# Two value passes in place of three, and the softmax's denominators on GpSimd, in a forgetting-attention stage

## The chip, the cores and the metric

The kernel runs on one core of a Trainium2 chip. The metric is the device time of one execution in microseconds, the median of several runs. TensorE (PE in the rows; its weight loads are PEld), VectorE (DVE), ScalarE (ACT), GpSimd (POOL) and the DMA queue of SyncE (SP) each work through their own list of instructions in order and wait for each other by semaphores.

## The reference, cut to what matters

The program is a two-layer trunk over 1024 tokens of width 1024: layer 0 mixes with forgetting attention (8 heads of 64) beside a causal pooling, layer 1 with RWKV-7, and each is followed by a SwiGLU FFN. The change is in the attention of layer 0 alone:

```python
logits = (jnp.einsum('bhqd,bhkd->bhqk', q_i, k).astype(jnp.float32) * scale
          + c_i[..., :, None] - cum[..., None, :])
causal = key_pos[None, :] <= q_pos[:, None]
p = jax.nn.softmax(jnp.where(causal, logits, -1e30), axis=-1)
return jnp.einsum('bhqk,bhkd->bhqd', p.astype(v.dtype), v)
...
attn = attn * jax.nn.sigmoid(og)
```

So of each head the kernel needs the numerator (weights times values), the denominator (the sum of the weights over the keys), and the output gate.

## The kernel before, in words

Everything is kept with channels on the 128 partitions and tokens on the free axis, in two halves of 512 tokens. Matrix products are made from float32 operands split into a high part and the remainder (`part`, `load_part`: ScalarE casts the high part, VectorE subtracts), and three passes hi·hi, hi·lo, lo·hi (`mm3`, lines 163 to 165).

`fox` is layer 0's mixer. It takes heads in pairs: `p` is the pair (0 to 3) and `a` the head in it, so there are eight heads, called here by (p, a). For each head `attend(p, a)` (line 525) goes through 12 steps: the half `hq` of the queries (0 or 1) and the key block `j` of 128 keys (4 blocks for half 0, 8 for half 1). On the blocks of the diagonal only part of the 512 queries is needed, so a step is 512, 384, 256 or 128 columns wide. A step has two parts:

- `scores` (line 531): two or three matmuls write the logits to a PSUM tile `s`; ScalarE takes the exponential into `pt` (line 543), casts the high part `ph` (line 546, in `copy_to`, line 121), and VectorE subtracts to get `pl` (line 547). `pt`, `ph` and `pl` have two buffers each.
- `values` (line 550), one step later: three matmuls add to the PSUM tile `o`: VH·ph (line 556), VH·pl (557), VL·ph (558). VH holds the high parts of the values on 64 of the 128 columns (`own`) and ones on the other 64 (`oth`); VL holds their low parts and zeros. So the 64 other rows of `o` collect the sum of the weights, the denominator.

After the last block of a half, `values` finishes it (lines 562 to 566): logarithm of the denominator (ScalarE), plus the gate's logarithm (VectorE), exponential of the negative (ScalarE), times the numerator (VectorE) into `y[p][hq]`.

While head (p, a) attends, other work is woven in by `weave` (line 217): `assemble` and `maxima` of the next head, and a filler. The filler is the projections of the next pair (`prep`) when a is 0; the pooling groups and the output gate (`pool_group`, `gate`) when a is 1; and for p = 3 the output projection (`oproj_early`). The weights of the weave only set the order in which the program records the work; a scheduler with its own costs then sets the order on each engine. Scratch tiles are taken in turn from five buffers (`tmp`), and the PSUM tile `t` (shared with `head_mean`, `assemble` and `maxima`) has one buffer.

GpSimd has almost no work: memsets, some of them of VH and VL at the start (lines 386 to 390), and small copies and sums on 16 columns in `pool_group` (lines 592, 595, 608, 609).

Of the kernel before, what the change touches and what calls it, by code (L numbers as in the profile page):

```python
# [9 lines left out]
F32 = mybir.dt.float32  # L10
# [6 lines left out]
P = 128  # L17
# [63 lines left out]
def rd(ap):  # L81
    return ap.bitcast(F32)
# [231 lines left out]
def fox(k, ins, H, hpool, xpools, y, then, r_att):  # L314
# [64 lines left out]
    KB = [ap_.tile([P, S], F32R, tag=f"KB{a}", name=f"KB{a}") for a in range(2)]  # L379
    QB = [ap_.tile([P, S], F32R, tag=f"QB{a}", name=f"QB{a}") for a in range(2)]  # L380
    VH = [ap_.tile([P, 8, P], F32R, tag=f"VH{a}", name=f"VH{a}") for a in range(2)]
    VL = [ap_.tile([P, 8, P], F32R, tag=f"VL{a}", name=f"VL{a}") for a in range(2)]
    for a in range(2):
        own = slice(64 * a, 64 * a + 64)
        oth = slice(64 - 64 * a, 128 - 64 * a)
        nc.gpsimd.memset(QB[a][oth].bitcast(F32), 0.0)
        nc.gpsimd.memset(KB[a][oth].bitcast(F32), 0.0)
        nc.gpsimd.memset(KB[a][64 - 64 * a:72 - 64 * a].bitcast(F32), 1.0)
        nc.gpsimd.memset(VH[a][:, :, oth].bitcast(F32), 1.0)
        nc.gpsimd.memset(VL[a][:, :, oth].bitcast(F32), 0.0)  # L390

# [82 lines left out]
    def assemble(p, a):  # L474
# [17 lines left out]
        nc.scalar.copy(VH[a][:, :, own], pvb)  # L492
        nc.vector.tensor_tensor(VL[a][:, :, own], pvb, rd(VH[a][:, :, own]), ALU.subtract)
        yield 2
# [30 lines left out]
    def attend(p, a):  # L525

        steps = [(a, hq, j) for hq in range(2) for j in range(4 * hq + 4)]
        live = []
        out = {}

        def scores(a, hq, j):
# [8 lines left out]
            if diag:  # L540
                nc.tensor.matmul(s[:, 0:P], identR, maskTR, start=False, stop=True)
            pt = ap_.tile([P, HN], F32, tag="pt", name=nm(k, "pt"), bufs=2)
            nc.scalar.activation(pt[:, 0:w], s[:, 0:w], AF.Exp, bias=ncumT[:, j, h:h + 1])
            ph = ap_.tile([P, HN], F32R, tag="ph", name=nm(k, "ph"), bufs=2)
            pl = ap_.tile([P, HN], F32R, tag="pl", name=nm(k, "pl"), bufs=2)
            copy_to(k, CE[2], ph[:, 0:w], pt[:, 0:w])
            nc.vector.tensor_tensor(pl[:, 0:w], pt[:, 0:w], rd(ph[:, 0:w]), ALU.subtract)
            return a, hq, j, q0, w, ph, pl

        def values(a, hq, j, q0, w, ph, pl):  # L550
            nj = 4 * hq + 4
            if j == 0:
                out[a, hq] = pst(k, "o", 2)
            o = out[a, hq]
            oo = o[:, q0 - hq * HN:HN]
            nc.tensor.matmul(oo, VH[a][:, j], ph[:, 0:w], start=(j == 0), stop=False)
            nc.tensor.matmul(oo, VH[a][:, j], pl[:, 0:w], start=False, stop=False)
            nc.tensor.matmul(oo, VL[a][:, j], ph[:, 0:w], start=False, stop=(j == nj - 1))
            if j == nj - 1:
                own = slice(64 * a, 64 * a + 64)  # L560
                oth = slice(64 - 64 * a, 128 - 64 * a)
                den = tmp("den")[:, 0:HN]
                nc.scalar.activation(den[own], o[oth], AF.Ln)
                nc.vector.tensor_tensor(den[own], den[own], y[p][hq][own], ALU.add)
                nc.scalar.activation(den[own], den[own], AF.Exp, scale=-1.0)
                nc.vector.tensor_tensor(y[p][hq][own], o[own], den[own], ALU.mult)
            return 3 * w / HN

        for st in steps:
            live.append(scores(*st))  # L570
            yield 2 * live[-1][4] / HN + 0.3
            if len(live) > 1:
                yield values(*live.pop(0))
        for l in live:
            yield values(*l)

    halo = ap_.tile([P, 4, 16], F32, tag="halo", name="halo")
# [974 lines left out]
```

## Time and profile before

| | |
|---|---|
| median of 3 runs | 2701.54 us (2696.48 to 2703.55) |
| the profiled execution | 2699.03 us |
| its span, first to last instruction | 2697.2 us |
| TensorE busy | 2633.8 us, 98% of the span |
| VectorE busy | 1724.3 us, 64% |
| ScalarE busy | 1301.9 us, 48% |
| GpSimd busy | 50.6 us, 2% |
| granted TensorE clock | 0.993 |

The profile is of one execution. A busy time is a union of the instructions' spans; matmuls overlap each other in it, so the price of a matmul is read as the distance from its start to the next one's start. The attention of layer 0 runs from 88 us to 463 us of the span, some 47 us a head.

### The profile page before, as it was taken

What the parts mean: (1) busy time and instruction counts of PE and PEld (TensorE: products, weight loads), DVE (VectorE), ACT (ScalarE), POOL (GpSimd) and SP (SyncE); (2) the same over time, 40 slices, a digit from 0 to 9 for tenths busy, and PEclk for the clock granted to TensorE, in tenths of its full rate; (3) what the DMA queues carried; (4) which work ended last, traced back from release to release, by engine and by line L of the source; (5) the groups of instructions that cost most, each with busy time, mean ns of one, the idle gap of its engine ahead of it and who ended that gap; (6) DMA issues with size and microseconds to landing.
All of it is one profiled execution on the core that took longest, in us unless ns stands there. A gap on an engine that the chain in (4) does not pass through costs nothing.

```text
span 2697.2 us, 40269 instructions
## 1 busy us (share of the span) xinstructions
PE 2633.8 (98%) x15368; PEld 2080.5 (77%) x15368; DVE 1724.3 (64%) x2940; ACT 1301.9 (48%) x2299; POOL 50.6 (2%) x139
## 2 busy tenths in 40 slices
PE   8999999999999999999999999999999999999999
PEld 6787878788888777777777677777777778888887
DVE  8777684654446655975995685469768856634443
ACT  7555564442224765534634466664445444332232
POOL 1000000000001000000000000000000000000000
PEclk9999999999999999999999999999999999999999
DMA  4111131233333546424523534454344336333333
GB/s 136 58 52 55 44 98 48 83 97 96 96 98 114 168 162 191 129 82 123 160 87 100 194 101 161 160 182 128 91 141 134 93 100 199 109 98 94 98 98 94
DMA packets 170817, 307.03 MB, mean 114 GB/s; under 512 B 18928, under 2 KB 25968, under 8 KB 170624
## 3 DMA queue, kind: packets, MB, share of 16 engines
q1 hardware_dynamic: 156800, 279.29, 33.6%
q10 hardware_dynamic: 13824, 25.17, 2.5%
q8 instruction: 120, 1.97, 0.3%
q14 instruction: 73, 0.60, 0.1%
HBM read 257.96 MB, written 46.43 MB: 113 GB/s over the span
## 4 chain that ended last, share of the span: by engine, by line
PE 77%; DVE 14%; DMA 3%; ACT 3%; issue 2%; SPq 0%; DVEq 0%; ACTq 0%
PE mm L163 16%; PE mm L164 16%; PE mm L165 16%; PE fm L163 6%; PE fm L164 5%; PE fm L165 5%; DVE wlo L152 2%; PE mm L175 1%; DVE nu L1108 1%; DVE pd L1106 1%; DMA wraw<-in_wu_dram 1%; DVE ZL L1064 1%; ACT whi L151 1%; PE o L1173 1%; PE s L1161 1%
## 5 line engine op out<-in xcount | busy, mean ns | idle before, releaser
L151 ACT CAST whi<-wraw 128x512 fp32r<-128x512 f32 x738 | 453.7, 617 | 867.4 <-PE mm L164 478.7
L152 DVE TENSOR_TENSOR wlo<-wraw,whi 128x512 fp32r<-128x512 f32 x738 | 501.3, 684 | 449.6 <-ACT whi L151 441.1
L163 PE MATMUL mm<-hh,whi 128*128 128x512 f32 x864 | 344.1, 400 | 6.2 <-ACT hh L355 6.1
L165 PE MATMUL mm<-hh,wlo 128*128 128x512 f32 x864 | 338.4, 392 | 0.0
L164 PE MATMUL mm<-hl,whi 128*128 128x512 f32 x864 | 337.9, 392 | 0.0
L163 PE MATMUL mm<-uh,whi 128*128 128x512 f32 x728 | 283.6, 391 | 0.9 <-DVE x L1317 0.9
L165 PE MATMUL mm<-uh,wlo 128*128 128x512 f32 x728 | 283.1, 390 | 1.0 <-DVE wlo L152 1.0
L164 PE MATMUL mm<-ul,whi 128*128 128x512 f32 x728 | 283.2, 390 | 0.0
L163 PE MATMUL fm<-h1h,whi 128*128 128x512 f32 x528 | 220.2, 417 | 14.8 <-DVE sg L726 9.9
L164 PE MATMUL fm<-h1l,whi 128*128 128x512 f32 x528 | 210.3, 398 | 0.1
L165 PE MATMUL fm<-h1h,wlo 128*128 128x512 f32 x528 | 209.5, 397 | 0.5 <-DVE wlo L152 0.5
L163 PEld LDWEIGHTS mm<-hh,whi 128*128 128x128 f32 x864 | 162.3, 188 | 43.4 <-ACT hh L355 7.8
L165 PEld LDWEIGHTS mm<-hh,wlo 128*128 128x128 f32 x864 | 162.5, 188 | 34.4 <-issue 0.2
L164 PEld LDWEIGHTS mm<-hl,whi 128*128 128x128 f32 x864 | 162.7, 188 | 33.1 <-DVE hl L260 1.7
L163 PE MATMUL fm<-hh,whi 128*128 128x512 f32 x416 | 170.9, 411 | 3.3 <-ACT hh L259 2.3
L164 PE MATMUL fm<-hl,whi 128*128 128x512 f32 x416 | 164.9, 396 | 0.2 <-DVE hl L260 0.2
L165 PE MATMUL fm<-hh,wlo 128*128 128x512 f32 x416 | 164.6, 396 | 0.0
L163 PEld LDWEIGHTS mm<-uh,whi 128*128 128x128 f32 x728 | 136.5, 188 | 34.6 <-issue 3.5
L164 PEld LDWEIGHTS mm<-ul,whi 128*128 128x128 f32 x728 | 136.6, 188 | 30.9 <-issue 1.1
L165 PEld LDWEIGHTS mm<-uh,wlo 128*128 128x128 f32 x728 | 136.7, 188 | 30.1 <-DVE wlo L152 1.8
L705 DVE TENSOR_TENSOR x<-mm,x 128x512 f32<-128x512 f32 x96 | 66.3, 692 | 119.3 <-PE mm L165 119.2
L163 PEld LDWEIGHTS fm<-h1h,whi 128*128 128x128 f32 x528 | 100.6, 191 | 47.1 <-DVE sg L726 12.2
(338 smaller groups left out, 4645.4 us busy)
## 6 DMA issues: line engine op xcount, KB each, us to landing
wraw<-in_wg_dram SPq DMA_DIRECT2D x176, 256.0 KB, 2.8
wraw<-in_wu_dram SPq DMA_DIRECT2D x176, 256.0 KB, 2.7
wraw<-in_wd_dram SPq DMA_DIRECT2D x176, 256.0 KB, 2.7
wraw<-in_w_in_dram SPq DMA_DIRECT2D x52, 256.0 KB, 2.9
x<-in_xT_dram SPq DMA_DIRECT2D x32, 256.0 KB, 4.6
x<-x SPq DMA_DIRECT2D x32, 256.0 KB, 3.3
wraw<-in_w_k_dram SPq DMA_DIRECT2D x32, 256.0 KB, 2.8
wraw<-in_w_v_dram SPq DMA_DIRECT2D x32, 256.0 KB, 3.0
```

Source lines behind the costliest of these rows:

```text
L151: k.nc.scalar.copy(hi[0:p, 0:n], raw[0:p, 0:n])
L152: k.nc.vector.tensor_tensor(lo[0:p, 0:n], raw[0:p, 0:n], rd(hi[0:p, 0:n]), ALU.subtract)
L163: nc.tensor.matmul(out, wh, xh, start=(first and i == 0), stop=False)
L164: nc.tensor.matmul(out, wh, xl, start=False, stop=False)
L165: nc.tensor.matmul(out, wl, xh, start=False, stop=(last and i == n - 1))
L175: k.nc.tensor.matmul(out[n * q:n * q + n], w[:, n * j:n * j + n], xs[j], start=c == 0, stop=c + g == len(xs), tile_position=(0, n * q))
L705: nc.vector.tensor_tensor(X[half][m], o, X[half][m], ALU.add)
L1064: nc.vector.tensor_tensor(ZL[h][HS[1 - h], i, bs], s4[HS[1]], self.msk[HS[1]].rearrange("p a t -> p (a t)").unsqueeze(1).broadcast_to([64, ...
L1106: nc.vector.tensor_tensor(pv, nu[:, j + 1:32, j:j + 1].broadcast_to([P, n, j]), nu[:, j:j + 1, 0:j].broadcast_to([P, n, j]), ALU.mult)
L1108: nc.vector.tensor_tensor(nu[:, j + 1:32, 0:j], nu[:, j + 1:32, 0:j], pv, ALU.add)
L1161: nc.tensor.matmul(z[HS[h], i], ZL[h][:, i, c, 0:64], SV[h][:, i, c], start=True, stop=True)
L1173: nc.tensor.matmul(sp[HS[h], i], BK[h][:, i, c], uv[h][:, i], start=True, stop=True)
```

## The change

The tile VL is gone. VH now holds the high parts of the values on `own` and their low parts on `oth` (both from the same transposes, by the same two instructions). Two passes, VH·ph and VH·pl, then give the products with the high part on the rows `own` of `o` and those with the low part on `oth`.

The denominators are summed elsewhere. The exponential of key block 0 goes to a tile `da` (two buffers, tag of its own) that is also the accumulator; for each later block GpSimd adds `pt` to it in place (10 sums a head). At the end of a half, `finish` splits the accumulator into two parts (ScalarE cast, VectorE subtraction), copies the low half of `o` to the rows `own` (ScalarE), adds it to the high half (VectorE), sums the accumulator over the keys by two matmuls with a matrix of equal entries into the PSUM tile `t`, and goes on as before with logarithm, gate, exponential and product. `finish` is taken up again one step after it was begun, so that its matmuls stand among the next steps. It takes four scratch tiles from `tmp`, where one was taken.

```diff
     VH = [ap_.tile([P, 8, P], F32R, tag=f"VH{a}", name=f"VH{a}") for a in range(2)]
-    VL = [ap_.tile([P, 8, P], F32R, tag=f"VL{a}", name=f"VL{a}") for a in range(2)]
...
-        nc.gpsimd.memset(VH[a][:, :, oth].bitcast(F32), 1.0)
-        nc.gpsimd.memset(VL[a][:, :, oth].bitcast(F32), 0.0)
...
         nc.scalar.copy(VH[a][:, :, own], pvb)
-        nc.vector.tensor_tensor(VL[a][:, :, own], pvb, rd(VH[a][:, :, own]), ALU.subtract)
+        nc.vector.tensor_tensor(VH[a][:, :, oth], pvb, rd(VH[a][:, :, own]), ALU.subtract)
...
-            pt = ap_.tile([P, HN], F32, tag="pt", name=nm(k, "pt"), bufs=2)
+            if j == 0:
+                pt = den[a, hq] = ap_.tile([P, HN], F32, tag="da", name=nm(k, "da"), bufs=2)
+            else:
+                pt = ap_.tile([P, HN], F32, tag="pt", name=nm(k, "pt"), bufs=2)
...
             nc.vector.tensor_tensor(pl[:, 0:w], pt[:, 0:w], rd(ph[:, 0:w]), ALU.subtract)
+            if j:
+                d = den[a, hq][:, q0 - hq * HN:]
+                nc.gpsimd.tensor_tensor(d, d, pt[:, 0:w], ALU.add)
...
             nc.tensor.matmul(oo, VH[a][:, j], ph[:, 0:w], start=(j == 0), stop=False)
-            nc.tensor.matmul(oo, VH[a][:, j], pl[:, 0:w], start=False, stop=False)
-            nc.tensor.matmul(oo, VL[a][:, j], ph[:, 0:w], start=False, stop=(j == nj - 1))
+            nc.tensor.matmul(oo, VH[a][:, j], pl[:, 0:w], start=False, stop=(j == nj - 1))
             if j == nj - 1:
-                own = slice(64 * a, 64 * a + 64)
-                oth = slice(64 - 64 * a, 128 - 64 * a)
-                den = tmp("den")[:, 0:HN]
-                nc.scalar.activation(den[own], o[oth], AF.Ln)
-                nc.vector.tensor_tensor(den[own], den[own], y[p][hq][own], ALU.add)
-                nc.scalar.activation(den[own], den[own], AF.Exp, scale=-1.0)
-                nc.vector.tensor_tensor(y[p][hq][own], o[own], den[own], ALU.mult)
+                ends.append(finish(a, hq, o, den[a, hq]))
             return 3 * w / HN
+
+        def finish(a, hq, o, d):
+
+            own = slice(64 * a, 64 * a + 64)
+            oth = slice(64 - 64 * a, 128 - 64 * a)
+            dh, dl = (ap_.tile([P, HN + 16], F32R, tag="tmp", name=nm(k, "dd"), bufs=k.tmpbufs)[:, 0:HN] for _ in range(2))
+            part(k, (dh, dl), d)
+            low = tmp("low")[:, 0:HN]
+            nc.scalar.copy(low[own], o[oth])
+            num = tmp("num")[:, 0:HN]
+            nc.vector.tensor_tensor(num[own], o[own], low[own], ALU.add)
+            yield 2
+            t = pst(k, "t", 1)
+            nc.tensor.matmul(t, onesR, dh, start=True, stop=False)
+            nc.tensor.matmul(t, onesR, dl, start=False, stop=True)
+            nc.scalar.activation(low[own], t[own], AF.Ln, scale=64.0)
+            nc.vector.tensor_tensor(low[own], low[own], y[p][hq][own], ALU.add)
+            nc.scalar.activation(low[own], low[own], AF.Exp, scale=-1.0)
+            nc.vector.tensor_tensor(y[p][hq][own], num[own], low[own], ALU.mult)
+            yield 0
 
         for st in steps:
             live.append(scores(*st))
             yield 2 * live[-1][4] / HN + 0.3
+            if ends and next(ends[0], None) is None:
+                ends.pop()
             if len(live) > 1:
                 yield values(*live.pop(0))
         for l in live:
             yield values(*l)
+        for e in ends:
+            yield from e
```

On TensorE the scheduler's list loses the 96 instructions of line 558 and gains the 32 of the two new lines. The end of the second half of head (0, 0), where head (0, 1) begins, stood so before (`o` of the last key block, then the first scores `s` of the next head and a projection `mm`):

```order
L163 MATMUL mm_1268<-hh_392,whi_1219 128x512
L164 MATMUL mm_1268<-hl_393,whi_1219 128x512
L165 MATMUL mm_1268<-hh_392,wlo_1220 128x512
L556 MATMUL o_1072<-ph_1303,VH_109 128x128
L557 MATMUL o_1072<-pl_1304,VH_109 128x128
L558 MATMUL o_1072<-ph_1303,VL_111 128x128
L538 MATMUL s_1329<-QA_104,KA_102 128x512
L539 MATMUL s_1329<-QB_108,KB_106 128x512
L541 MATMUL s_1329<-maskTR,identR 128x128
```

The same place on TensorE now:

```order
L163 MATMUL mm_1271<-hh_386,whi_1223 128x512
L164 MATMUL mm_1271<-hl_387,whi_1223 128x512
L165 MATMUL mm_1271<-hh_386,wlo_1224 128x512
L561 MATMUL o_1069<-ph_1306,VH_109 128x128
L562 MATMUL o_1069<-pl_1307,VH_109 128x128
L579 MATMUL t_1334<-dd_1324,onesR 128x512
L580 MATMUL t_1334<-dd_1325,onesR 128x512
L536 MATMUL s_1341<-QA_104,KA_102 128x512
L537 MATMUL s_1341<-QB_108,KB_106 128x512
L539 MATMUL s_1341<-maskTR,identR 128x128
```

The two sums over the keys (`t`) stand straight behind the last value pass here; the scores and projections around them keep their places.

On VectorE, at the same place, before (`den` is the denominator's scratch tile, `x` the gate, `wlo` a weight's low part, `av` the next pair's values):

```order
L547 TENSOR_TENSOR pl_1304<-pt_1301,ph_1303 128x128
L443 TENSOR_TENSOR av_1327<-mm_1268,rs_98 128x512
L152 TENSOR_TENSOR wlo_1466<-wraw_1467,whi_1465 128x512
L564 TENSOR_TENSOR den_1322<-den_1322,x_503 64x512
L566 TENSOR_TENSOR x_503<-o_1072,den_1322 64x512
L547 TENSOR_TENSOR pl_1336<-pt_1333,ph_1335 128x512
```

And VectorE there now (`dd` are the parts of the accumulator `da`):

```order
L549 TENSOR_TENSOR pl_1307<-pt_1304,ph_1306 128x128
L260 TENSOR_TENSOR dd_1325<-da_1005,dd_1324 128x512
L441 TENSOR_TENSOR av_1332<-mm_1271,rs_98 128x512
L152 TENSOR_TENSOR wlo_1478<-wraw_1479,whi_1477 128x512
L576 TENSOR_TENSOR num_1330<-o_1069,low_1328 64x512
L582 TENSOR_TENSOR low_1328<-low_1328,x_497 64x512
L549 TENSOR_TENSOR pl_1348<-da_1345,ph_1347 128x512
L584 TENSOR_TENSOR x_497<-num_1330,low_1328 64x512
```

Two instructions came in, the split of the accumulator and the sum `num`, and the next head's `pl` moved ahead of the last product.

On GpSimd, in the heads (1, 0) and (1, 1), there was before only the pooling groups' small work:

```order
L592 COPY pu_2433<-halo 128x16
L595 COPY halo<-pu_2433 128x16
L608 TENSOR_TENSOR x_2442<-pa_2437,fc 128x16
L609 TENSOR_TENSOR x_2442<-x_2442,pu_2433 128x16
L592 COPY pu_2558<-halo 128x16
```

And now, from the end of the first of the two heads into the second:

```order
L552 TENSOR_TENSOR da_2022<-da_2022,pt_2265 128x384
L552 TENSOR_TENSOR da_2022<-da_2022,pt_2296 128x256
L552 TENSOR_TENSOR da_2022<-da_2022,pt_2321 128x128
L552 TENSOR_TENSOR da_2362<-da_2362,pt_2406 128x384
L552 TENSOR_TENSOR da_2362<-da_2362,pt_2443 128x256
L614 COPY pu_2481<-halo 128x16
L552 TENSOR_TENSOR da_2362<-da_2362,pt_2514 128x128
L617 COPY halo<-pu_2481 128x16
L630 TENSOR_TENSOR x_2490<-pa_2485,fc 128x16
```

The sums stand between the pooling groups' instructions, which keep their order among themselves. From the first FFN on, each engine's order is that of before.

## Rows read from the trace of the kernel before

**Rows 1.** The page, part 1: busy us (share of the span) and instructions of each engine.

```profile
PE 2633.8 (98%) x15368; PEld 2080.5 (77%) x15368; DVE 1724.3 (64%) x2940; ACT 1301.9 (48%) x2299; POOL 50.6 (2%) x139
```

**Rows 2.** Busy times by stretch: heads (0,0), (0,1), (1,1), (2,1), (3,1).

```profile
core 0: us, PE busy (x) PEld busy (x) DVE busy (x) ACT busy (x) POOL busy (x), PEclk, DMA share, GB/s
88.00:137.00 49.00, 48.40 (x239) 39.11 (x239) 32.41 (x69) 31.02 (x58) 0.20 (x1) 1.00 0.12 39
137.00:185.00 48.00, 46.73 (x227) 38.29 (x227) 37.13 (x78) 26.89 (x51) 2.77 (x5) 1.00 0.21 68
...
232.00:281.00 49.00, 47.92 (x231) 38.88 (x230) 40.02 (x83) 25.80 (x48) 3.75 (x8) 1.00 0.21 68
...
328.00:375.00 47.00, 45.17 (x221) 36.05 (x220) 38.27 (x79) 30.14 (x57) 0.30 (x3) 1.00 0.25 79
...
418.00:463.00 45.00, 45.00 (x215) 37.55 (x214) 19.20 (x31) 20.47 (x36) 0.10 (x1) 1.00 0.16 47
```

**Rows 3.** TensorE's waits, 88 to 463 us: us in total, times, longest.

```profile
PE mm L163 <- ACT pp L586: 1.6, 5, 0.4
PE o L557 <- DVE pl L547: 1.2, 5, 0.4
```

**Rows 4.** Line 558 by source: duration ns min/median/max, first and last start, forms.

```profile
L558 PE MATMUL o<-ph,VL x96: 275/364/398, 91.2 to 464.9; 128*128 128x512 f32 x48, 128*128 128x384 f32 x16, 128*128 128x256 f32 x16, 128*128 128x128 f32 x16
```

**Rows 5.** Timeline of TensorE, line 558 in each width: start us, us, instruction.

```profile
152.35 0.39 PE L558 MATMUL o<-ph,VL 128*128 128x512 f32 x1
152.59 0.22 PE L509 MATMUL s<-KA,QA 128*128 128x128 f32 x1
...
345.27 0.33 PE L558 MATMUL o<-ph,VL 128*128 128x384 f32 x1
345.44 0.28 PE L509 MATMUL s<-KA,QA 128*128 128x256 f32 x1
...
348.82 0.28 PE L558 MATMUL o<-ph,VL 128*128 128x256 f32 x1
348.94 0.34 PE L509 MATMUL s<-KA,QA 128*128 128x384 f32 x1
...
352.97 0.28 PE L558 MATMUL o<-ph,VL 128*128 128x128 f32 x1
353.08 0.44 PE L538 MATMUL s<-QA,KA 128*128 128x512 f32 x1
```

**Rows 6.** Timeline of TensorE: a `t` matmul behind a 128-column one.

```profile
97.67 0.45 PE L276 MATMUL t<-ep,onesR 128*128 128x512 f32 x1
97.95 0.39 PE L538 MATMUL s<-QA,KA 128*128 128x512 f32 x1
```

**Rows 7.** VectorE and ScalarE groups, 88 to 470 us: busy us, mean ns | idle before.

```profile
L564 DVE TENSOR_TENSOR den<-den,x 64x512 f32<-64x512 f32 x16 | 11.0, 686 | 7.8 <-ACT den L563 7.7
...
L259 ACT CAST hh<-x 128x512 fp32r<-128x512 f32 x16 | 9.4, 616 | 1.4 <-DVE x L566 0.8 <-PE mm L164 0.4
```

**Rows 8.** Timeline of GpSimd and VectorE at two of GpSimd's sums.

```profile
78.74 0.56 DVE L512 CUSTOM_DVE_ANT_0 s<-s,bc 128x384 f32<-128x384 f32 x1
...
78.96 0.22 POOL L608 TENSOR_TENSOR x<-pa,fc 128x16 f32<-128x16 f32 x1 [1.01 <-PE s L511]
...
157.91 0.68 DVE L547 TENSOR_TENSOR pl<-pt,ph 128x512 fp32r<-128x512 f32 x1
...
158.07 0.60 POOL L608 TENSOR_TENSOR x<-pb,fc 128x16 f32<-128x16 f32 x1 [1.60 <-DVE pb L602]
```

**Rows 9.** GpSimd's 64x256 copies by source and in the timeline, VectorE beside them.

```profile
L1149 POOL COPY SV<-S x8: 397/402/632, 1035.7 to 1984.9; 64x256 f32<-64x256 f32 x8
...
1035.70 0.85 POOL L1149 COPY SV<-S 64x256 f32<-64x256 f32 x2 [8.15 <-PE mm L164]
...
1036.33 0.77 DVE L152 TENSOR_TENSOR wlo<-wraw,whi 128x512 fp32r<-128x512 f32 x1 [1.35 <-ACT whi L151]
```

**Rows 10.** Timeline of TensorE at the end of head (2,1).

```profile
372.65 0.44 PE L557 MATMUL o<-pl,VH 128*128 128x384 f32 x1 [0.41 <-DVE pl L547]
```

## What the change should do to the time, predicted before it ran

> **What bounds the kernel now.** I read the page's busy shares first: TensorE is busy 98% of the span, VectorE 64% [rows 1]. That share says little about one stage, so next come the busy times by stretch, one stretch a head [rows 2]. The column to look at is the gap between a stretch's length and TensorE's busy time. In head (0,0) it is 0.6 us of 49, in (3,1) nothing of 45. In the three heads where pooling is woven in, (0,1), (1,1) and (2,1), it is 1.1 to 1.8 us. TensorE's waits in the stage are five entries that come to under 5 us; the longest in sum are 1.6 us for the pooling's split and 1.2 us for `pl` [rows 3]. So TensorE's own work sets the pace of the attention, and a matmul taken out is worth its place in the queue. The second column to look at is VectorE's: 32.41 us of 49 in (0,0) and 19.20 of 45 in (3,1), but 37.13 of 48 in (0,1), 40.02 of 49 in (1,1) and 38.27 of 47 in (2,1) [rows 2]. In these three heads VectorE has only 9 to 11 us left, and the change puts more on it, directly and by what GpSimd does beside it.
>
> **What is removed.** Line 558 runs 96 times: 48 of 512 columns, 16 each of 384, 256 and 128 [rows 4]. Its price is the distance to the next start, not its span of 0.39 us: 0.24, 0.17, 0.12 and 0.11 us [rows 5]. 48 x 0.24 + 16 x (0.17 + 0.12 + 0.11) = 11.5 + 6.4 = 17.9 us, all on the path, since TensorE waits so little. The memsets of VH and VL go too; they stand at the start on an engine that is busy 50.6 us in all [rows 1] and I cost that at nothing.
>
> **What TensorE gets.** Two matmuls of 512 columns for each of 16 half-heads: 32. In a run of wide ones each takes 0.24 us [rows 5]; a `t` matmul that stands behind a 128-column one takes 0.28 [rows 6]. In the new order most pairs stand behind wide projections, three straight behind a 128-column pass. The ends are 7.7 and 9.0 us; I take 8.2. So TensorE's own work falls by 17.9 - 8.2 = 9.7 us, with 8.9 to 10.2 as bounds.
>
> **What VectorE and ScalarE get.** Each half has two more instructions on VectorE (the split of the accumulator and `num`) and two more on ScalarE (cast, copy); the rest of `finish` answers to the old ending, and the values' low parts are still one subtraction. At 0.69 us on VectorE and 0.62 on ScalarE [rows 7] that is 2.8 and 2.5 us a head. ScalarE, at 25.80 to 31.02 us of 47 to 49 in these heads [rows 2], takes it. On VectorE the cover is its idle time: ample in the heads (p,0) and in pair 3, 9 to 11 us in the three named.
>
> **What GpSimd's sums cost.** A head has 10 sums over 3584 columns (384, 256, 128, four times 512, then 384, 256, 128). No row has a wide one. The nearest rows: a sum of 16 columns takes 0.22 us when nothing disturbs it [rows 8], a copy of 256 columns, with one input, 0.40 [rows 9]. The difference is 0.18 us for 240 columns, 0.75 ns a column for one input. If the second input costs nothing, 512 columns take 0.22 + 496 x 0.75 ns = 0.6 us; if it costs as much again, 0.96; if I charge the copy's whole time to its columns and double it, 1.6. I take 0.96, because doubling goes by the slope of the nearest row: 3584 x 1.5 ns + 10 x 0.2 = 7.4 us a head, on an engine that is free. GpSimd's time itself is hidden: a sum has until the exponential two steps on, which needs its `pt` buffer.
>
> What isn't hidden is the meeting with VectorE. At 78.96 us the 16-column sum ran beside line 512, which reads PSUM and one SBUF tile, and took its 0.22. At 158.07 the same sum ran beside `pl` (line 547, two SBUF inputs) and took 0.60: `pl` ended at 158.59, the sum at 158.67 [rows 8]. It goes the other way too: line 152, two SBUF inputs, began at 1036.33 while the second of two GpSimd copies was reading, and took 0.77, where such an instruction takes 0.68 [rows 8, 9]. So the two engines exclude each other on such instructions. It was small so far because GpSimd's instructions were.
>
> The Trainium skill says the same more strongly and against this change: in "SBUF — State Buffer", section "Who interferes with whom", a VectorE instruction with two SBUF inputs and a GpSimd instruction that reads SBUF lock a shared port, and the second fully blocks until the first ends. The rows agree for GpSimd's wait (0.60 for 0.22); for VectorE's they show only 0.09 us, at a copy that had 0.2 us left. The skill's "GPSIMD Engine Reference", section 3.1, gives 4497 ns for a two-input sum of 2048 columns; a quarter, 1.12 us, is an estimate from that page; by it a head's sums take about 8 us, and the total below would lose about half a microsecond.
>
> How much of 7.4 us a head does VectorE lose? Lower end nothing (it always has a one-input instruction ready), upper end all of it. Lines 547, 152 and 260 have two SBUF inputs, line 512 and everything else that reads PSUM don't, and VectorE is also idle at times; with nothing nearer to either end I take the middle, 3.7 us. Then the three heads need 37.13, 40.02 and 38.27 plus 2.8 + 3.7 = 43.6, 46.5 and 44.8 us, in stretches that would be 1.2 us shorter: 46.8, 47.8 and 45.8. It fits, but at 93 to 98%, and VectorE works in order: a late `pl` or `wlo` is a wait on TensorE. Already before, at the end of (2,1), where TensorE has almost no filler, it waited 0.41 us for `pl` [rows 10]. I put 1 us of new waits on (0,1), 2 on (1,1) and 2 on (2,1): 5 us in all, 0 to 12 as bounds.
>
> **The new waits of the ending.** The sum over the keys needs the last GpSimd sum, then ScalarE's cast (0.62), then VectorE's subtraction (0.69). Where its matmuls stand straight behind the last value pass, as in the order shown for (0,0), the second has 14 matmuls, some 2.8 us, between the last scores and itself, and the chain (exponential, small sum, cast, subtraction) takes about as long. Behind it in TensorE's queue stand the next head's first scores. I put 0.3 us on each of three such places: 1 us, with 0 to 3 as bounds. Elsewhere four or more wide matmuls are between, and I cost it at nothing; if a sum is late there, ScalarE's queue stops at the cast, with exponentials and weight casts behind it.
>
> **The sum.** 9.7 - 5 - 1 = 3.7 us less. The profiled execution took 2699.03 us (span 2697.2), so 2695.3 against itself. It lies 2.5 us under the median of 2701.54, from where the same step gives 2697.8. I forecast 2696.5.
>
> **The rivals.**
>
> *Full gain.* VectorE's queue absorbs it all: it has 9 to 11 us left even in the three busy heads, and a result that comes ahead of its matmul may come later for free. Then 9.7 us come out: 2689.3 to 2691.8, say 2691. Against it: 93 to 98% in three heads.
>
> *VectorE becomes the bound.* If the lock takes all of GpSimd's time from VectorE, and with the upper price of 1.6 us a sum, VectorE loses 7.4 to 12 us a head, and the three a = 1 heads need at least 37.13 + 2.8 + 7.4 = 47.3, 50.2 and 48.5 us against 46.8, 47.8 and 45.8, plus the idle time that the order forces on it (line 564 alone waited 7.7 us in the stage [rows 7]). With 6 to 9 us more a head this is 18 to 27 us, less the 9.7: some 13 us slower, 2712. The turning point is a loss of about 5 us a head on VectorE in those three heads. For it: the two-way wait in the rows. Against it: half of VectorE's instructions don't take part.
>
> *No gain, the slots stay.* Where TensorE waits for `pl` anyway, as at the end of (2,1) [rows 10], a pass less changes nothing, and the ending's chain comes on top; spread over all heads the time would stay at 2700 or so. Against it: waits of under 5 us in the stage.
>
> **How the numbers follow.** About 0.3%, 8.1 us, is what a measurement of this kernel can tell from no change. Forecast, with its neighbours down to no gain (2694 to 2702): 0.60. Full gain: 0.27; it passes the bound by a little, so I count it as faster. VectorE the bound: 0.13. Hence faster 0.27, same 0.60, slower 0.13. The third rival lies in the forecast's range. The range goes from the full gain, 2690, up towards the slower case as far as leaves out about 2 in 10: 2708.
>
> **What would show it.** TensorE's matmuls fall by 64; a head's stretch gets shorter by about 1.2 us in the heads (p,0). GpSimd's sums of 512 columns read near 1 us where undisturbed and up to 0.7 longer beside two-input instructions. Instructions of lines 547 and 152 (new numbers) show spans over 0.69 where a sum runs. In TensorE's waits, those for `pl`, `wlo` and `dd` grow to some 5 us in the heads (0,1), (1,1) and (2,1). If VectorE's spans don't grow, full gain is right; if its busy share in these heads passes 97% and they get longer than before, the slower rival is. The forecast is wrong in kind if the difference lies outside 88 to 475 us.

## The result, and the profile after

The changed kernel takes 2712.03 us in the median (2710.0 to 2719.1), the kernel before 2701.59: ratio 1.0047, 95% interval 1.0034 to 1.0060. It is slower, by 10.4 us. The forecast was 2696.5 us, with a range of 2690 to 2708, so the time lies outside it and on the other side.

Page after, part 1, busy us of each engine (answers to [rows 1]):

```profile
PE 2641.4 (97%) x15304; PEld 2079.5 (77%) x15304; DVE 1768.4 (65%) x2972; ACT 1319.1 (49%) x2331; POOL 130.1 (5%) x215
```

TensorE has its 64 matmuls less. VectorE, with 32 instructions more, is busy 44 us longer. GpSimd has 80 us more.

Busy times by stretch of the kernel after: heads (0,0), (0,1), (1,1), (2,1), (3,1), the cuts moved with the work (answers to [rows 2]):

```profile
core 0: us, PE busy (x) PEld busy (x) DVE busy (x) ACT busy (x) POOL busy (x), PEclk, DMA share, GB/s
89.00:139.00 50.00, 48.62 (x232) 38.15 (x232) 38.13 (x75) 33.56 (x64) 11.05 (x11) 1.00 0.12 36
139.00:187.00 48.00, 46.04 (x215) 35.94 (x214) 41.51 (x82) 28.15 (x52) 11.86 (x15) 1.00 0.22 68
...
235.00:285.00 50.00, 47.60 (x224) 37.61 (x223) 44.79 (x87) 26.98 (x49) 14.14 (x18) 1.00 0.20 63
...
334.00:382.00 48.00, 44.14 (x210) 34.30 (x209) 41.47 (x79) 31.90 (x60) 11.98 (x15) 1.00 0.23 72
...
428.00:473.00 45.00, 45.00 (x214) 37.55 (x213) 24.98 (x36) 22.05 (x41) 10.00 (x12) 1.00 0.16 48
```

The gap between length and TensorE's busy time was 0.6 to 1.8 us; now it is 1.4 in (0,0), 2.0, 2.4 and 3.9 in the three heads with pooling, and still nothing in (3,1). VectorE is nowhere full: 41.5 of 48, 44.8 of 50, 41.5 of 48, at most 90%.

TensorE's waits, 88 to 490 us, after (answers to [rows 3]; its five entries came to 4.9 us, the twelve of now to 14.4):

```profile
PE s L536 <- DVE mx L510: 3.7, 6, 0.9
PE o L562 <- DVE pl L549: 3.1, 8, 0.5
...
PE mm L163 <- DVE x L1339: 1.2, 3, 0.8
...
PE t L580 <- DVE dd L260: 0.4, 1, 0.4
```

Before, the wait of the scores for `mx`, the maxima of the next head, was this:

```profile
PE s L538 <- DVE mx L512: 0.9, 2, 0.7
```

`mx` and `pl` are VectorE's results. The wait for `mx` has grown most, from 0.9 to 3.7 us, and it is not in a step of the ending at all; the wait for `pl` has grown from 1.2 to 3.1 us. The third kind to look at is line 163's for the mixer's last output, which before had no counterpart: it stands behind the end of the last half.

Timeline of VectorE and GpSimd after, at one step of head (0,0):

```profile
105.42 1.29 POOL L552 TENSOR_TENSOR da<-da,pt 128x512 f32<-128x512 f32 x1 [4.54 <-ACT pt L545]
...
105.62 1.63 DVE L484 TENSOR_TENSOR QB<-aq,QA 64x512 fp32r<-64x512 f32 x1
...
107.18 0.67 DVE L549 TENSOR_TENSOR pl<-pt,ph 128x512 fp32r<-128x512 f32 x1
```

The sum runs from 105.42 to 106.71. Line 484, two inputs in SBUF, is 1.63 us long in place of 0.68: it ends 0.54 us behind the sum. `pl` stands behind it in VectorE's queue. In most steps it is `pl` itself that is held: in 21 of the 32 steps with a sum of 512 columns it takes over 0.72 us, up to 1.31. VectorE's groups of line 549, 88 to 480 us, after (busy us, mean ns of one):

```profile
L549 DVE TENSOR_TENSOR pl<-pt,ph 128x512 fp32r<-128x512 f32 x32 | 31.5, 983 | 5.8 <-ACT ph L121 4.9
...
L549 DVE TENSOR_TENSOR pl<-da,ph 128x512 fp32r<-128x512 f32 x16 | 11.0, 686 | 4.9 <-ACT ph L121 4.9
```

The control is in the kernel itself. Blocks with a sum (`pl<-pt`) take 983 ns in the mean, first blocks without one (`pl<-da`) 686. GpSimd's sums of 512 columns, same stretch:

```profile
L552 POOL TENSOR_TENSOR da<-da,pt 128x512 f32<-128x512 f32 x32 | 41.9, 1309 | 125.1 <-ACT pt L545 122.5 <-DVE wlo L152 1.4 <-DVE hl L260 1.2
```

Equal matmuls of the two traces stand 10.1 us apart at 430 us of before and still at 850, so the loss is in the attention (some 1.5 us of it is a stretch at the lower clock at 288 us). Behind that the profiled executions differ by stretches at the lower clock, which came before the change too (the profile of after is of an execution of 2719.1 us), and I don't read the change there.

### The profile page after: what moved, and what is told of

Same layout as the page of the kernel before. It is cut to its first block, busy times and chain, and to the rows that moved or that the text cites. A ratio compares the mean times of both kernels' runs of the same rounds, so it can differ in the third digit from the quotient of the medians.

```text
span 2717.3 us, 40391 instructions
## 1 busy us (share of the span) xinstructions
PE 2641.4 (97%) x15304; PEld 2079.5 (77%) x15304; DVE 1768.4 (65%) x2972; ACT 1319.1 (49%) x2331; POOL 130.1 (5%) x215
## 4 chain that ended last, share of the span: by engine, by line
PE 77%; DVE 15%; ACT 3%; issue 3%; DMA 2%; SPq 0%; DVEq 0%; ACTq 0%
PE mm L163 16%; PE mm L164 15%; PE mm L165 15%; PE fm L163 7%; PE fm L164 6%; PE fm L165 6%; DVE wlo L152 2%; PE mm L175 1%; PE s L1078 1%; DVE nu L1130 1%; DVE pd L1128 1%; DMA wraw<-in_wu_dram 1%; PE o L1195 1%; PE s L1183 1%; PE s L1189 1%
## 5 line engine op out<-in xcount | busy, mean ns | idle before, releaser
L163 PEld LDWEIGHTS fm<-h1h,whi 128*128 128x128 f32 x528 | 101.2, 192 | 46.3 <-DVE sg L748 10.7
```

The source lines that it names most:

```text
L163: nc.tensor.matmul(out, wh, xh, start=(first and i == 0), stop=False)
```

## Experiments

The first theory, A: GpSimd's sums hold VectorE's two-input instructions in all heads. Rivals: B, the ending's chain and the one buffer of `t`; C, the new order; D, VectorE's load. GpSimd has 80 sums (10 a head; the 72 in two of the expectations is a slip). All kernels were run beside the kernel before, whose median was 2699.8 to 2701.3 us; ratios are to it, with 95% intervals.

**No sums.**

```diff
-            if j:
-                d = den[a, hq][:, q0 - hq * HN:]
-                nc.gpsimd.tensor_tensor(d, d, pt[:, 0:w], ALU.add)
...
```

> This kernel is the changed one without GpSimd's 72 sums: the denominators come from the first block of keys alone, with a small constant added under the logarithm so that it stays finite (these are the parts of the computation that are changed). The two value passes, the split of the accumulator, its two matmuls and the rest of finish stay. Before is 2701.6 us, the changed kernel 2712.0. Theory A, GpSimd's sums lengthen and delay VectorE's two-input instructions, pl above all, in every head: without them the saving of the third pass comes out, 2691 to 2696 us, and pl reads 0.69 us again in place of 1.24 to 1.30. Rival B, the chain at the end of a half and the single buffer of t cost it: the same instructions stand in the queues, so part of the loss stays, 2699 to 2708. Rival C, the new order of the matmuls or VectorE's two extra instructions a half cost it: 2706 to 2712.

2701.27 us, 1.0004 [0.9995, 1.0012]. Without the sums the kernel is 10.7 us faster (some 60 of TensorE's matmuls in the attention also changed places; the next run has no such difference). But nothing is gained over the kernel before: `pl` is back at 688 ns, TensorE's wait for `mx` is 1.0 us, and the saving still doesn't come out. So A is only half, and B's time (2699 to 2708) is borne out.

**Sums that nobody reads.**

```diff
+                db = ap_.tile([P, HN], F32, tag="db", name=nm(k, "db"), bufs=2)
-                nc.gpsimd.tensor_tensor(d, d, pt[:, 0:w], ALU.add)
+                nc.gpsimd.tensor_tensor(db[:, 0:w], d, pt[:, 0:w], ALU.add)
...
```

> This kernel is the one without sums plus GpSimd instructions of the same kind, count and widths as the changed kernel's, that read the first block and the new block and write a tile that nobody reads. Denominators come from the first block alone, with the small constant, as there. The order on TensorE, VectorE and ScalarE is that of the kernel without sums, row by row, so the difference of the two is what GpSimd's instructions cost the others while nobody waits for their results. Theory A: 10 to 18 us above the kernel without sums, at 2706 to 2712. Rival B, the loss is the chain that waits for the last sum: within 3 us of the kernel without sums. Rival C: both alike at 2706 to 2712.

2714.62 us, 1.0050 [1.0036, 1.0064]: 13.3 us above the kernel without sums, in the same order on the three other engines. Here nobody waits for a sum's result, so its price is not the chain behind the last sum. VectorE's busy time in the attention grows from 287.9 to 309.7 us. One more rival is that a sum holds its block's buffer `pt`, for which the exponential two steps on must wait. The traces speak against it: in this one none of the exponentials that ScalarE had to wait for begins within 0.4 us behind the end of a sum, in the changed kernel's one of 52. So what is left is what the sums do to VectorE.

Where does it cost time? Equal matmuls of this trace fall behind those of the trace without sums, both at the full clock there, by 6 us over the three heads with pooling and by 4 us over the heads (p,0), and not at all in (3,1).

**Writes in place of sums.**

```diff
-                nc.gpsimd.tensor_tensor(d, d, pt[:, 0:w], ALU.add)
+                nc.gpsimd.memset(d, 1.0)
```

> In the changed kernel each of GpSimd's sums is replaced by one instruction that writes 1.0 to the same columns of the accumulator and reads nothing, so the denominators are wrong. The chain stays: finish waits for GpSimd's last write. Theory A, it is GpSimd's reading of two inputs that VectorE's two-input instructions wait for: pl at 0.69 us, time as without sums, 2691 to 2697 us. A variant of A, any access of GpSimd to the same memory does it: pl above 0.9 us and 2700 us or more. Rival B: the chain is there, so 2699 to 2708. Rival C: 2706 to 2712.

2701.44 us, 1.0000 [0.9992, 1.0009]: as without sums. But these writes don't wait for the exponential, and the trace has them in a row behind the first block's `pl`, not beside the later ones. So the run says nothing of what a write beside `pl` would do.

**Sums on VectorE.**

```diff
-                nc.gpsimd.tensor_tensor(d, d, pt[:, 0:w], ALU.add)
+                nc.vector.tensor_tensor(d, d, pt[:, 0:w], ALU.add)
```

> The changed kernel with the 72 sums on VectorE in place of GpSimd, everything else as it is. Each sum is then about 0.69 us for 512 columns, 0.2 to 0.5 for the narrow ones, 5 us a head on VectorE, which is busy 38 to 45 us in heads of 46 to 50 us with pooling and 25 to 38 in the others. Theory A: a sum on VectorE takes half of what GpSimd's takes away, and it does not stand ahead of pl, which comes first in the queue: 2694 to 2703 us, below the changed kernel. Rival D, VectorE's load is what makes pl and the maxima late, whoever causes it: 5 us a head more and 2706 to 2716. Rival C: 2706 to 2716 too, but with pl of 0.69 us starting on time.

2707.03 us, 1.0020 [1.0011, 1.0030], 4 us over A's upper end and at D's lower. VectorE's busy time in the attention tells more. The windows run from 86 us to the same matmul in each kernel (480 us of before). Without sums, after, and with the sums on VectorE:

```profile
86.00:478.00 392.00, 382.12 (x1791) 304.27 (x1790) 287.86 (x581) 236.35 (x435) 7.05 (x24) 1.00 0.18 57
```

```profile
86.00:490.00 404.00, 388.09 (x1794) 305.14 (x1793) 313.41 (x585) 237.13 (x435) 88.30 (x104) 1.00 0.18 55
```

```profile
86.00:484.00 398.00, 386.75 (x1795) 303.48 (x1794) 324.17 (x665) 235.44 (x435) 8.40 (x24) 1.00 0.17 56
```

GpSimd's sums add 25.6 us to VectorE's busy time and cost 10.7 us; its own sums add 36.3 and cost 5.8. Load alone (D) isn't the measure: a sum on VectorE waits behind `pl`, one on GpSimd comes ahead of it.

**The removal alone.** The next two take the change apart without sums.

```diff
...
-                ends.append(finish(a, hq, o, den[a, hq]))
...
+                nc.scalar.activation(den_[own], o[oth], AF.Ln, scale=0.0, bias=rd(onesR)[oth, 0:1])
+                nc.vector.tensor_tensor(den_[own], den_[own], y[p][hq][own], ALU.add)
+                nc.scalar.activation(den_[own], den_[own], AF.Exp, scale=-1.0)
+                nc.vector.tensor_tensor(y[p][hq][own], o[own], den_[own], ALU.mult)
...
```

> The removal alone: the kernel without sums, and also without finish's split of the accumulator, its two matmuls, copy and num; the half ends with the old kernel's four instructions on ScalarE and VectorE, as in the kernel before. Left out of the computation: the denominators (a constant takes their place under the logarithm) and the values' low parts. TensorE has 96 matmuls less than before and none more, 17.9 us by rows 4 and 5. Theory E, TensorE paces the stage but the ending's additions cost more than their matmuls: the removal gives its price, 2682 to 2686 us, 15 us under the kernel without sums. Rival F, the passes stood where TensorE would wait anyway, for ph, pl and the split of other operands, so a part of the 17.9 us turns into waits whatever the ending does: 2688 to 2694 us, and the waits of the stage grow by 4 us or more over the 4.9 us of before.

2685.84 us, 0.9947 [0.9935, 0.9960]: 15.1 us faster. In the trace the stretch from 86 us to that same matmul is 378 us long, not 394. So TensorE does set the pace, and the passes give nearly their price (E). The 2 or 3 us that lack to 17.9 are within what the medians leave uncertain; TensorE's waits come to 6.1 us for the 4.9 of before, where F asked for 4 more.

**The ending alone.**

```diff
-                den = tmp("den")[:, 0:HN]
-                nc.scalar.activation(den[own], o[oth], AF.Ln)
...
+                ends.append(finish(a, hq, o, y[p][hq]))
...
```

> The addition alone: the kernel before, with its three passes and without sums, but with the changed kernel's finish at the end of each half: split, two matmuls into t, copy and num, gate. The split reads the gate's tile in place of an accumulator, so the denominators are wrong. TensorE has 32 matmuls more than before, 8.2 us by my sum. Theory E, the ending also holds the one buffer of t, two of five temporary tiles and two instructions more on each of ScalarE and VectorE: 2713 to 2718 us, 12 to 17 us above before, with waits at lines that use t or read temporary tiles. Rival F, the ending costs its matmuls and little else: 2708 to 2711 us.

2712.70 us, 1.0045 [1.0032, 1.0057]: 11.8 us slower with three passes, between F's 2711 and E's 2713. On two passes the same ending costs 2701.27 - 2685.84 = 15.4 us. It was priced at 9.2.

**The sums over the keys in a buffer of `o`.**

```diff
...
-            t = pst(k, "t", 1)
+            t = pst(k, "o", 2)
...
```

> The kernel without sums, with the two matmuls of finish writing to a buffer of o (two buffers) in place of the single buffer of t, for which the norms' means, the value transposes and the maxima's transposes also queue. Denominators from the first block, as there (2701.3 us). If the single buffer of t is what the loss beside the sums comes from: 2696 to 2699 us, and the extra time before matmuls into t goes (it is 3 us over before's in that kernel). If not: 2700 to 2704 us, or more, as o's next half waits for the logarithm.

2701.55 us, 1.0001 [0.9992, 1.0010]. The single buffer of `t` is not what the ending costs, or `o` takes as much.

**Weaving by two passes.**

```diff
...
-            return 3 * w / HN
+            return 2 * w / HN
...
```

> The kernel without sums, with the weight that values gives the weaving set from three passes to two (the code still counts three), so that less filler is woven per step and more is left behind it. Denominators from the first block, as there (2701.3 us). Rival C, the interleaving no longer fits the steps: 2695 to 2699 us. If the order matters little: 2700 to 2703. If the filler is what covers the latency of exponential, cast and split: 2704 or more, with more waits for ph and pl.

2700.63 us, 0.9998 [0.9989, 1.0008], without sums. Over 400 matmuls stand elsewhere, and the time is the same, so C has lost its ground. It is one other order, and not that of before.

**The ending's matmuls alone**, on the kernel with the removal alone; `dz` is a tile of zeros.

```diff
...
+            t = pst(k, "t", 1)
+            nc.tensor.matmul(t, onesR, dz, start=True, stop=False)
+            nc.tensor.matmul(t, onesR, dz, start=False, stop=True)
...
```

> The kernel with the removal alone (2685.8 us), plus two matmuls of 512 columns into t at the place where finish has them, 32 in all, on a tile of zeros that is there from the start; nobody reads their result. Left out: denominators and low parts, as in that kernel. If these matmuls cost their slots and no more: 7.3 us by the spacing of wide ones in its trace, so 2692 to 2694 us. If the single buffer of t makes them dearer even when nobody reads it: 2695 to 2698. The kernel without sums, which has the whole ending, is at 2701.3.

2695.92 us, 0.9976 [0.9966, 0.9986]: 10.1 us over the removal alone, at the upper case. The trace's attention is only 7 us longer (385 for 378), which is the slots. The medians are uncertain by 3 us, so 7 to 10 is what can be said.

**The ending's instructions on ScalarE and VectorE alone.**

```diff
-            nc.tensor.matmul(t, onesR, dh, start=True, stop=False)
-            nc.tensor.matmul(t, onesR, dl, start=False, stop=True)
-            nc.scalar.activation(low[own], t[own], AF.Ln, scale=64.0, bias=rd(onesR)[own, 0:1])
+            nc.scalar.activation(low[own], num[own], AF.Ln, scale=0.0, bias=rd(onesR)[own, 0:1])
...
```

> The kernel without sums, also without the two matmuls into t: the split, copy, num and gate stay on ScalarE and VectorE, and the logarithm takes a constant (so the denominators are left out). TensorE has the 96 matmuls less and none more, as in the kernel with the removal alone (2685.8 us). If the ending's extra instructions on ScalarE and VectorE hide, as the prediction said of all but three heads: 2685 to 2688 us. If they make other things late: 2689 to 2694. What then lacks to the 15.4 us between 2685.8 and 2701.3, after the matmuls' own 7 us and this, is the chain through both: the end of the last half, and t's buffer held until the logarithm has read it.

2691.93 us, 0.9962 [0.9949, 0.9974]: 6.1 us over the removal alone. In the trace the attention is 7 us longer, about half of it at the lower clock, so 4 to 6 us is what can be said. They don't hide, although ScalarE and VectorE are far from full. By the medians 10.1 and 6.1 make 16.2, where both together cost 15.4, which leaves nothing for the chain through both. By the traces' attention, without the stretch at the lower clock, 7 and some 4 make 11 of 14 us (392 for 378), which leaves 3. So the chain costs something between nothing and 3 us, and the runs can't tell what. One place of it is seen in TensorE's waits of the kernel without sums:

```profile
PE mm L163 <- DVE x L1336: 1.3, 3, 0.8
```

That is the output projection behind the last half. The half's product needs two matmuls, a logarithm, a sum and an exponential, and no other work is left to fill in.

**One copy per step, then two, then a wide one.** These ask whether GpSimd must read two inputs to hold VectorE. All are the kernel without sums, plus copies that nobody reads.

```diff
...
+                nc.gpsimd.tensor_copy(db[:, 0:w], pt[:, 0:w])
...
```

> The kernel whose sums nobody reads (2714.6 us; without sums 2701.3), with a GpSimd copy of the new block in place of each sum: one input from memory, not two. If what holds VectorE's two-input instructions is any reading by GpSimd, for as long as it lasts: copies of 512 columns last 0.7 to 0.9 us by the 0.40 of 256 columns in rows 9, about two thirds of a sum's 1.3, so 2707 to 2711 us, with pl above 0.69 us in most steps. If it takes two inputs: 2700 to 2703 us, with pl at 0.69.

2703.45 us, 1.0008 [0.9999, 1.0017], `pl` at 687 ns: by its numbers "it takes two inputs". But a copy lasts 638 ns and begins with the cast, which lasts 620; it is as good as over when `pl` begins. The run couldn't tell.

```diff
...
                 nc.gpsimd.tensor_copy(db[:, 0:w], pt[:, 0:w])
+                nc.gpsimd.tensor_copy(db[:, 0:w], pt[:, 0:w])
...
```

> The kernel with one GpSimd copy per step (2703.5 us), with each copy made twice, one after the other. The order on TensorE, VectorE and ScalarE is that of the kernel without sums (2701.3 us), row by row. One copy of 512 columns lasts 0.64 us and was over by the time pl began, so it told nothing of one input against two; two last 1.28 us, as long as a sum (1.31), and the second lies beside pl. If any reading by GpSimd holds pl: pl of the later blocks near 0.98 us, as beside sums, and 2710 to 2715 us. If it takes a second input: pl at 0.69 and 2702 to 2706 us.

2707.15 us, 1.0023 [1.0014, 1.0032], between the two cases. GpSimd's second copies and `pl` beside them:

```profile
L553 POOL COPY db<-pt 128x512 f32<-128x512 f32 x32 | 29.9, 935 | 1.8
...
L552 POOL COPY db<-pt 128x512 f32<-128x512 f32 x32 | 20.5, 641 | 117.8 <-ACT pt L545 117.8
```

```profile
L549 DVE TENSOR_TENSOR pl<-pt,ph 128x512 fp32r<-128x512 f32 x32 | 24.3, 760 | 7.4 <-ACT ph L121 6.6
```

Between the two copies `pl` often goes first, and then the copy waits: 935 ns for 641. Whoever comes first holds the other.

```diff
...
+                nc.gpsimd.tensor_copy(db[:, 0:1], pt[:, 0:1])
+                nc.gpsimd.tensor_copy(db[:, 0:2 * w], rd(QA[a][:, 0:2 * w]))
...
```

> The kernel without sums (2701.3 us) with one GpSimd copy per step that is twice as wide as a sum, 1024 columns for 512, from a tile that is there anyway, started when the exponential is done; nobody reads it. It has one input, and by 0.64 us for 512 columns it lasts about 1.2 us, as long as a sum of two inputs, without a break in the middle where pl could go first. If any reading by GpSimd holds pl for as long as the instruction lasts: pl of the later blocks at 0.9 to 1.0 us, and 2709 to 2714 us. If it takes a second input: pl at 0.69 to 0.76 and 2702 to 2706 us.

2710.88 us, 1.0045 [1.0032, 1.0057]. VectorE's `pl`:

```profile
L549 DVE TENSOR_TENSOR pl<-pt,ph 128x512 fp32r<-128x512 f32 x32 | 33.4, 1045 | 8.7 <-ACT ph L121 8.0
```

One input read by GpSimd is enough, if it lies beside `pl` without a break: `pl` at 1045 ns and 9.6 us lost, nearly as with the sums. The 9.6 us are not all the copies' hold on VectorE: ScalarE's next `QA` waits 2.3 us in all for copies that still read it, and some 50 of TensorE's matmuls changed places. The length of `pl` doesn't depend on either.

**A sum behind `pl`.** The first try:

```diff
...
+                nc.gpsimd.tensor_copy(gs, rd(pl[:, 0:1]))
                 nc.gpsimd.tensor_tensor(d, d, pt[:, 0:w], ALU.add)
```

> The changed kernel (2712.0 us) with a GpSimd copy of one column of pl ahead of each sum, so that the sum begins when pl is done and not when the exponential is. Nothing is left out; the order on TensorE, VectorE and ScalarE is the changed kernel's, row by row. Theory A', a sum costs because it lies beside pl, which the values wait for next: pl back at 0.69 us, and 2702 to 2707 us; what is left of the sums' 10.7 us is what they do to other two-input instructions. Theory A'', a sum costs VectorE the same wherever it lies: 2709 to 2715 us, with the lengthening moved from pl to the next two-input instructions.

2712.58 us, 1.0047 [1.0033, 1.0061]; it changed nothing, and can't decide. The scheduler put the read behind the sum of its step, and `pl` stayed at 959 ns. The second try ties the sum to it by the data:

```diff
+                nc.gpsimd.tensor_copy(pt[:, 0:1], pt[:, 0:1])
                 nc.gpsimd.tensor_tensor(d, d, pt[:, 0:w], ALU.add)
```

> The changed kernel (2712.0 us) with GpSimd writing one column of the new block onto itself ahead of each sum. This write has to wait until pl has read the block, and the sum has to wait for the write, so a sum begins behind pl, which the run with a read of pl did not bring about. Nothing is left out. Theory A', a sum costs because it lies beside pl, which the values wait for next: pl back at 0.69 us, and 2702 to 2707 us; what is left of the sums' 10.7 us is what they do to other two-input instructions (weights' low parts, projections' splits). Theory A'', a sum costs VectorE the same wherever it lies: 2709 to 2716 us, with the lengthening moved from pl to those others.

2723.20 us, 1.0091 [1.0078, 1.0104], slower than either case. VectorE's groups, 88 to 480 us, and TensorE's longest wait, 86 to 501 us:

```profile
L152 DVE TENSOR_TENSOR wlo<-wraw,whi 128x512 fp32r<-128x512 f32 x50 | 41.8, 840 | 11.4 <-ACT whi L151 11.1
L549 DVE TENSOR_TENSOR pl<-pt,ph 128x512 fp32r<-128x512 f32 x32 | 22.0, 687 | 5.1 <-ACT ph L121 4.2
```

```profile
PE t L580 <- ACT dd L259: 5.5, 5, 1.3
```

`pl` is free, and the weights' low parts (line 152) are held in its place, at 840 ns for 686. The new loss is the ending's chain: the last sum comes later, the cast waits for it, and TensorE's `t` waits 5.5 us for the cast. Some 8 us of this trace's attention are lost to stretches at the lower clock (0.98 in the mean over it), which before's attention doesn't have. But all four executions lie at 2721.9 to 2730.0 us, so how much of the 23 us is the clock stays open. VectorE's busy time in the attention is 308.5 us, for 287.9 without sums: the sum costs VectorE something wherever it lies (A''), and a better place beside `pl` was paid for at the ending. How much each takes of the time stays open.

**The change in the heads (p,0) alone.**

```diff
...
-            if j == 0:
+            if j == 0 and not a:
...
+            if a:
+                nc.tensor.matmul(oo, VL[:, j], ph[:, 0:w], start=False, stop=(j == nj - 1))
...
```

> The whole change in the heads (p,0) alone; the heads (p,1), three of which have pooling woven in, keep the old three passes, the ones in VH and the old ending. Nothing is left out of the computation. The traces so far put 7.6 of the 10.3 us that GpSimd's sums cost into the heads (p,1), and the 2.1 us wait after the last half at (3,1). If so, the heads (p,0) alone gain 8.9 us of removed passes, pay 3.7 of matmuls into t, about 2.5 of locks and 2 to 3 of the ending: 2698 to 2703 us, the same as before. If the loss is spread evenly: half of the 11 us, 2705 to 2708.

2701.44 us, 1.0001 [0.9990, 1.0012]. As far as 3 us can be told, the change in these heads neither gains nor loses, as expected. By difference the loss comes with the other four heads; the change in those alone was not run. No version that computes everything beats the kernel before: even with free sums, the ending gives back what the passes save.

## Why the prediction was wrong, step by step

The account of the runs' medians: the removal -15.1 us, the ending's matmuls +10.1, its instructions on ScalarE and VectorE +6.1 (the two together 15.4), GpSimd's sums +10.7. With 15.4 that is +11.0, and 10.4 was measured. The forecast had -17.9 + 8.2 + 1 + 5 = -3.7. So the sign turned on three terms: 2.8 us less saved, 6.2 more for the ending, 5.7 more for the sums. Each median is uncertain by some 3 us. The sums' 10.7 lies inside the bounds of 0 to 12. The ending's 15.4 lies outside its own, 7.7 to 9.0 for the matmuls and 0 to 3 for the chain: that is the step that failed.

- *The removed passes* (17.9): 15.1 by the medians, 16 by the trace. The price from the distance to the next start was sound; whether "all on the path" was a little too much can't be told.
- *TensorE's new matmuls* (8.2): 7 by the trace, 10.1 by the medians. Right within what can be told.
- *What VectorE and ScalarE get*: the step that failed for the ending. I priced these 64 instructions by spare time, 9 to 26 us a head, and charged nothing outside the three heads with pooling, where they went into the 5 us of new waits. Alone they cost 6.1 us (some 4 by the trace). Both engines work in order, and a split or a copy that stands in front of a `pl`, a maximum or a cast makes it late, however idle the engine is later. That is the likely reason, but it is not shown: no run singles out one of them, and the scratch tiles, four for one, are a rival that no run separates. The step counted busy time, and idle time was no measure of the price.
- *The ending's chain* (1, bounds 0 to 3): between nothing and 3, inside the bounds, but I looked for it in the middle halves. It shows behind the very last half (1.2 us), where the filler is gone.
- *What GpSimd's sums take from VectorE* (3.7 us a head): 25.6 us over eight heads is 3.2. That it came out near is luck, since two errors cancel: a sum of 512 columns took 1.31 us, not 0.96 (inside the bounds), so a head's sums took 10.1 us and not 7.4, and VectorE lost a third of it and not half.
- *What that costs TensorE* (5 us, bounds 0 to 12): 10.7, inside the bounds. The forecast took new waits from VectorE's share coming near full, in three heads. The share never passed 90%, and the loss came all the same, 4 of 10 us of it in heads (p,0), where VectorE had 7 us or more left: a sum starts when the exponential ends, which is half a microsecond ahead of `pl`, so in two steps of three it hits the one instruction on which the next values wait. The turning point in the rival, full VectorE, was the wrong test.

The slower rival named 2712 us and the lock as cause, but its mechanism was VectorE as the bound; that the number came out is half luck. (Its upper price of 1.6 us a sum makes 11 us a head over 3584 columns, not 12.) "No gain" was wrong: the passes gave 15 us. Of the signs that I named, the 64 matmuls and the spans over 0.69 at line 549 (983 ns) and its neighbours came. Of the waits, the one for `pl` grew by 2 us and those for `wlo` and `dd` by next to nothing; the largest, for `mx`, I had not named. The shorter heads (p,0) and the busy share over 97% did not come.

The Trainium skill, in "SBUF — State Buffer", section "Who interferes with whom", says that a VectorE instruction with two SBUF inputs contends with a GpSimd instruction that reads SBUF, that the port they share is an exclusive lock, and that the order of issue decides who blocks. The traces agree on both counts: `pl` at 1045 ns beside a one-input copy, a copy at 935 behind `pl`. The prediction cited this section; what I made of it was an average over the head, where the order of the step decides who is first.

## What to carry to other kernels

Don't price an instruction added on a half-idle engine by the engine's spare time: look at what stands behind it in the queue, and run the added part alone, which shows its price at once. If GpSimd reads memory, ask at which moment it starts: released by the same event as a chain on VectorE, it got in ahead of the chain in two steps of three, and GpSimd instructions that end before VectorE's turn cost almost nothing (2 us for 80 copies, within what can be told from none). And do the removal and the addition separately before arguing about their sum.

## What the runs showed of the hardware

A GpSimd sum of two inputs and 512 columns took 1.29 to 1.31 us, one of 128 columns 0.46 at the least; a copy of 512 columns 0.62 undisturbed. A GpSimd copy of one input holds VectorE's two-input instructions as a sum does. The weight of a reading GpSimd instruction is in its place: 80 copies (0.64 us at 512 columns) that ended ahead of `pl` cost 2.2 us, 80 of twice the width (1.04 us at 1024), most of which lay beside `pl`, 9.6.
